# A hybrid decoder layer on one core: small transfers moved to another queue, one product at full width, the last heads laid between the products of the output projection

## The chip, the cores and the metric

One core of a Trainium2 chip runs one launch of the kernel. The metric is the device time of that launch in microseconds (us), the median of several runs. The kernel before takes 2108.51 us (median of 3 runs, 2108.4 to 2108.64).

## The reference, cut to what matters

Everything is fp32. The layer is FFN 1 (SwiGLU), a mixer, FFN 2 (SwiGLU), each behind an RMSNorm that is modulated by a conditioning vector, and a last RMSNorm. The sequence has 256 positions and the model 2048 features. Only the mixer is touched by the change. It has 8 heads of attention with a forget gate (FoX) and 8 heads of a gated delta rule (GDN) in chunks of 64 positions:

```python
def gated_delta_rule(q, k, v, g, beta):      # chunks of 64, n = 4 chunks
    ...
    lower = jnp.where(strict, jnp.einsum("bhnid,bhnjd->bhnij", kb, k) * decay, 0.0)
    t_inv = lax.linalg.triangular_solve(eye + lower, ...)
    u = t_inv @ vb
    w = t_inv @ (kb * jnp.exp(g)[..., None])
    a_intra = jnp.where(incl, jnp.einsum("bhnid,bhnjd->bhnij", q, k) * decay, 0.0)
    def step(state, inp):
        v_new = u_i - w_i @ state
        o = (q_i * jnp.exp(g_i)[..., None]) @ state + a_i @ v_new
        ...
def hybrid_mixer(h, w_in, w_out, ...):
    proj = h @ w_in
    ...
    return jnp.concatenate([o_f, o_g], axis=-1) @ w_out
```

## The kernel before, in words

**Weights.** All weights (674 blocks of 512 KB, eight 128x128 tiles each) come through one class, `Stream` (L68). `next` loads a block on SyncE's queue (L92, SP in the profile), ScalarE (ACT) rounds it to a high part `whi` (L95), and VectorE (DVE) subtracts for the low part `wlo` (L98). Three buffers of each kind go round. `mm` (L351) makes each product of two matmuls: `whi` by both halves of the activation (L352, 512 columns) and `wlo` by the high half (L353, 256 columns); in the mixer's input projection they are L555 to L557 and L568 to L570. Between these blocks the conditioning matrix is read in tiles of 1 MB (L203, `adat`, also on SyncE) and reduced on DVE (L205).

**Order of the work.** The program is written as a sequence of projections (a list of names, `ORDER`, L43: K a key head, G a GDN head, F a FoX head, Z and V row projections). The heads' chains (`solve`, `gdn`, `fox`) are generators: `tick` (L335) goes on with them between products when a planned time has passed, `finish` (L341) runs one to its end. The Tile scheduler then puts every engine's instructions in one fixed list; an engine runs its list in order, so an instruction that waits holds all behind it. That holds for a queue's transfers too.

**The mixer** (L517) first stores the residual stream `x` to DRAM in four transfers of 512 KB (L538, `xd<-x`), uses its space, and reads it back at the end (L542, `x_back`, `x<-xd`). `gates` (L585) stores the decay rows (L642). `row_of` (L650) reads one row broadcast to 128 partitions (L654, `rw<-rowd`, 24 times). `keys` (L689) makes the triangular factor `Ln` of each GDN head (L712). `solve` (L714) inverts the 16x16 diagonal blocks of four heads at once: 8 writes to DRAM (L725, `ld<-Ln`, 8 KB each), 8 broadcast reads (L730, `x<-ld`, 128 KB each), a memset on GpSimd (L734, POOL), 15 pairs of product and sum on DVE (L737, L738). It runs twice.

**`gdn`** (L748): for each of 4 chunks, a product of the packed `wq` with the state (L850), a subtraction (L851, `vz`), a product by `At` (L853), a state update (L857 to L862). `At` holds a_intra transposed, 128x128 for two chunks; L853 multiplies by 64 of its columns, into half of the output's partitions. Then copies of `po` (L866, L867, `orw`), a norm and gate (L875), two transposes (L880, `pot`), and the split to `oh` in high and low (L886, L887).

**The end of the mixer** (L988 to L1007): all chains are finished, `x` is read back, and the output projection runs: 16 output blocks of 128 features, each a sum over 16 heads (`ko`, L994). The first four blocks go together, in four PSUM banks, head by head (64 pairs of matmuls); the others follow one at a time. `residual` (L369, ends at L377) adds each to `x`.

Of the kernel before, what the change touches and what calls it, by code (L numbers as in the profile page):

```python
# [16 lines left out]
P = 128  # L17
D = 2048
T = 256
# [6 lines left out]
NH = 8  # L26
# [13 lines left out]
HIDX = 3  # L40
MORE = True
GAP = {"k": 1.0, "gdn": 1.0, "fox": 1.2}
ORDER = ("K3 K4 K5 K6 K7 Z0 G0 V0 F0 G1 F1 G2 F2 G3 F3 V1 Z1 G4 F4 G5 F5 G6 F6 G7 F7").split()  # L43
N_O = 17
MAGIC = 0x5F3759DF

# [63 lines left out]
def layer_kernel(ctx: ExitStack, tc: tile.TileContext, xt, c, adaw, cols, cst, w, out, order, dbg=None):  # L110
# [76 lines left out]
    def ada_col():  # L187

        i = ada_st["i"]
        if i >= len(ada_seq):  # L190
            return
        ada_st["i"] += 1
        m, j = ada_seq[i]
        q = m * KD + j
        if first_ada:
            t = first_ada.pop(0)
        else:
            t = adap.tile([P, D], F32, name="adat")
            if W.last is None:
                nc.sync.dma_start(t, adaw[i])  # L200
            else:
                with tc.issue_after(W.last):
                    nc.sync.dma_start(t, adaw[i])  # L203
        with W.behind(False):
            V.tensor_tensor_reduce(t, t, cs, 1.0, L("adab", q, 1), ALU.mult, ALU.add, mod[:, q : q + 1])  # L205
        if (m, j) in ada_done:
            ada_done[m, j]()
# [309 lines left out]
    def mixer():  # L517
# [16 lines left out]


        for q in range(4):
            with tc.issue_after(W.last):
                nc.sync.dma_start(xd[:, 4 * q : 4 * q + 4], x[:, 4 * q : 4 * q + 4])  # L538

        def x_back(q):  # L540
            with tc.issue_after(W.last):
                nc.sync.dma_start(x[:, 4 * q : 4 * q + 4], xd[:, 4 * q : 4 * q + 4])  # L542

        def spare(slot, n=2):
            return x[:, slot : slot + n].rearrange("p a t -> p (a t)")
# [39 lines left out]
        def gates(ps):  # L585

            yr = x[:, 8]
            A.copy(yr[R], ps[R])
            y, ny, e, em, t0, q = (x[:, j, : 2 * GR].rearrange("p (t r) -> p t r", t=2) for j in range(10, KD))
            coef = tiny.tile([P, GR], F32, name="coef", bufs=1)  # L590
            tc.keep_in_program_order(A.activation(coef, L("alog"), AF.Exp))
            V.tensor_scalar(coef, coef, -1.0, None, ALU.mult)
            yield 1.0
            pc = psf("pcol")
            pcv = pc[:, : 2 * GR].rearrange("p (t r) -> p t r", t=2)
            for t in range(2):
                PE.transpose(pcv[:, t], yr[R, t * P : (t + 1) * P], ident[R, :GR])
            both = lambda c_: c_.unsqueeze(1).to_broadcast([P, 2, GR])
            V.tensor_tensor(y, pcv, both(L("gbias")), ALU.add)
            V.tensor_tensor(y, y, both(C("sgn")), ALU.mult)  # L600
            V.scalar_tensor_tensor(ny, y, -1.0, y, ALU.mult, ALU.min)
            A.activation(e, ny, AF.Exp)
            V.tensor_scalar(em, y, 0.0, None, ALU.min)
            A.activation(em, em, AF.Exp)

            S = ny
            V.tensor_scalar(t0, e, 2.0, None, ALU.add)
            V.reciprocal(t0, t0)
            V.tensor_tensor(S, e, t0, ALU.mult)
            V.tensor_tensor(t0, S, S, ALU.mult)  # L610
            V.tensor_scalar(q, t0, 1.0 / 17.0, None, ALU.mult)
            for n in (15, 13, 11, 9, 7, 5, 3):
                V.scalar_tensor_tensor(q, q, 1.0 / n, t0, ALU.add, ALU.mult)
            V.scalar_tensor_tensor(q, q, 1.0, S, ALU.add, ALU.mult)
            V.tensor_scalar(y, y, 0.0, None, ALU.max)
            V.scalar_tensor_tensor(y, q, 2.0, y, ALU.mult, ALU.add)
            V.tensor_tensor(y, y, both(coef), ALU.mult)

            V.tensor_scalar(t0, e, 1.0, None, ALU.add)
            V.reciprocal(t0, t0)  # L620
            V.tensor_tensor(colS[:, :, 4], em[:, :, 16:24], t0[:, :, 16:24], ALU.mult)
            yield 6.0

            fox_, gdn_ = slice(0, NH), slice(NH, 2 * NH)
            pr = psf("prow")
            po = psf("pcum")
            pcs = po[:, : 6 * NH].rearrange("p (t q r) -> p t q r", t=2, q=3)
            for t in range(2):
                sl = slice(t * P, (t + 1) * P)
                PE.matmul(pr[:NH, T + t * P : T + (t + 1) * P], y[:, t, gdn_], C("tri64"), start=True, stop=True)  # L630
                PE.matmul(pr[:NH, sl], y[:, t, fox_], C("tri"), start=True, stop=(t == 0))
                if t:
                    PE.matmul(pr[:NH, sl], y[:, 0, fox_], L("ones"), start=False, stop=True)
            for t in range(2):
                PE.matmul(pcs[:, t, 1], C("tri64"), y[:, t, gdn_], start=True, stop=True)
                PE.matmul(pcs[:, t, 2], C("tru64"), y[:, t, gdn_], start=True, stop=True)
                PE.matmul(pcs[:, t, 0], C("tri"), y[:, t, fox_], start=True, stop=(t == 0))
                if t:
                    PE.matmul(pcs[:, t, 0], L("ones"), y[:, 0, fox_], start=False, stop=True)
            rt = x[:, 8:10].rearrange("p a t -> p (a t)")[:NH]  # L640
            A.copy(rt, pr[:NH])
            nc.sync.dma_start(rows, rt)  # L642
            V.tensor_copy(colS[:, :, 0:2], pcs[:, :, 0:2])
            A.activation(colS[:, :, 2:4], pcs[:, :, 1:3], AF.Exp)
            V.tensor_tensor(nbeg, colS[:, :, 4], colS[:, :, 2], ALU.mult)
            V.tensor_scalar(nbt, colS[:, :, 4], -1.0, None, ALU.mult)
            V.tensor_scalar(ng, colS[:, :, 1], -1.0, None, ALU.mult)
            yield 1.0

        def row_of(h, kind, tag):  # L650

            rb = m2p.tile([P, T], F32, name="rw", tag="rw" + tag)
            with tc.issue_after(W.last):
                nc.sync.dma_start(rb, rows[h : h + 1, kind * T : (kind + 1) * T].broadcast_to([P, T]))  # L654
            return rb

        bc = lambda c_: c_.unsqueeze(1).to_broadcast([P, 2, P])
# [56 lines left out]
        def solve(half):  # L714
# [7 lines left out]
            Lh = Ln[:, hs4].rearrange("p h t j -> p (h t) j")  # L722
            for b in range(8):
                r = slice(16 * b, 16 * b + 16)
                nc.sync.dma_start(ld[ht, b].rearrange("n r c -> r n c"), Lh[r, :, r])  # L725
            rows_ = x[:, ht]
            for b in range(8):
                r = slice(16 * b, 16 * b + 16)
                src = ld[ht, b].rearrange("n r c -> n (r c)").unsqueeze(0).to_broadcast([16, n, 256])
                nc.sync.dma_start(rows_[r], src)  # L730
            yield 9.0
            U = tmp.tile([P, n, 16], F32, name="u16", bufs=1)
            pr = tmp.tile([P, n, 16], F32, name="pr16", bufs=1)
# [14 lines left out]
        def gdn(h):  # L748
# [52 lines left out]
            for t in range(2):  # L801
# [3 lines left out]
            U = U2  # L805

            wq = m1p.tile([P, 2, 4, 64], F32, name="wq")
            V.tensor_tensor(wq[:, :, 1:3, :], q_[:, 0].rearrange("p (t c i) -> p t c i", t=2, c=2),
                            egb.rearrange("p (t c i) -> p t c i", t=2, c=2), ALU.mult)
            yield 1.4  # L810
            pu = pss("put")
# [19 lines left out]
                PE.matmul(pu[:, T + t * P : T + (t + 1) * P], kb[:, t], Ub[:, t], start=True, stop=True)  # L831
            u = m1p.tile([P, 2, P], F32, name="u")
            A.copy(uz[:64], pu[:64, :P])
            V.tensor_copy(wq[:, :, 0:4:3, :], pu[:, T:].rearrange("p (t c i) -> p t c i", t=2, c=2))
            A.copy(u.rearrange("p t i -> p (t i)"), pu[:, :T])


# [2 lines left out]
            for c_ in range(4):  # L840
# [5 lines left out]
                if c_ == 0:  # L846
                    new = uz
                else:
                    new = vz[:, c_ - 1]
                    PE.matmul(pc_, wq[:, t, 2 * ev : 2 * ev + 2].rearrange("p a i -> p (a i)"), st, start=True, stop=True)  # L850
                    V.tensor_sub(new[r], u[r, t], pc_[r])  # L851
                    yield 1.2
                PE.matmul(pc_[ro], At[:, t, 64 * ev : 64 * ev + 64], new, start=(c_ == 0), stop=True,  # L853
                          skip_group_check=True)
                if c_ < 3:
                    pst = pss("pst")
                    PE.matmul(pst[:, :P], kd[:, t], new, start=True, stop=True)  # L857
# [5 lines left out]
                    st = s2  # L863
            orw = m1p.tile([P, 2, P], F32, name="orw")
            pov = po.rearrange("p (t c d) -> p t c d", t=2, c=2)
            A.copy(orw[:64], pov[64:, :, 0])  # L866
            A.copy(orw[64:], pov[:64, :, 1])  # L867
            sso = tiny.tile([P, 2], F32, name="sso")
            for t in range(2):
                j1 = tmp.tile([P, P], BF16, name="j1")  # L870
# [114 lines left out]
            have_keys(h, first[1 + h])  # L985
        for name in ORDER:
            step(name[0], int(name[1]))
        for kind in chains:  # L988
            finish(kind, NH)
        for q in range(4):  # L990
            x_back(q)


        ko = [NH + h for h in range(4)] + list(range(NH)) + [NH + h for h in range(4, NH)]  # L994
        for js in [list(range(4))] + [[j] for j in range(4, KD)]:
            pj = [psn(i, "po") for i in range(len(js))]
            for i, k in enumerate(ko):
                for q, j in enumerate(js):
                    mm(pj[q], W.next("o", k, j), oh_[k], i == 0, i == KD - 1)
            for q, j in enumerate(js):  # L1000
                residual(pj[q], j, 5, False)
                sumsq_add(j)
# [139 lines left out]
```

## Time and profile before

| | us |
|---|---|
| median of 3 runs | 2108.51 |
| the profiled execution | 2112.91 |
| its span in the trace | 2111.1 |
| PE busy in the span | 2021.6 (96%) |
| DVE busy | 1564.3 (74%) |
| input projection and heads of the mixer | 806.6 to 1237.87 |
| output projection | 1237.87 to 1345.0 |

PE is TensorE's matmuls and PEld its weight loads, which overlap them; ACT is ScalarE, DVE VectorE, POOL GpSimd, SP SyncE. A row of the groups has line, engine, operation, output and inputs, shapes and count, then busy time and mean ns of one, then the idle time of the engine ahead of it and who ended it. A row of the timeline has the start, the length (both us), engine, line, operation, names, count, and in brackets the idle time before it and who ended that. The mean granted TensorE clock was 0.983 over the span. A row of the windows gives, for a stretch of the span in us, each engine's busy time with its instructions in brackets, the granted clock, and the load of the DMA engines.

### The profile page before, as it was taken

To read this page: it belongs to the slowest core of one execution; us is meant where nothing else is said; L and a number is where in the kernel's file an instruction comes from. 1 tells how busy PE (TensorE), PEld (TensorE's weight loads), DVE (VectorE), ACT (ScalarE), POOL (GpSimd) and SP (SyncE) were. 2 spreads that over 40 slices of the span, in tenths; PEclk is the share of its full clock that TensorE was granted. 3 is DMA by queue.
4 is the path that set the end of the run, shared out by engine and by line. 5 is a ranking of instruction groups with operands and counts; after the bars stand their busy time and mean duration, and the time that the engine had idled before them with its cause. 6 is when DMAs were issued, how large, how long until landed. Compare 5 with 4: busy or idle time off the path is not lost.

```text
span 2111.1 us, 33297 instructions
## 1 busy us (share of the span) xinstructions
PE 2021.6 (96%) x12914; PEld 1822.2 (86%) x12914; DVE 1564.3 (74%) x2387; ACT 1021.2 (48%) x1583; POOL 59.3 (3%) x62
## 2 busy tenths in 40 slices
PE   4999999999999998879999999899999999999997
PEld 4998999888888888769989988788888888888886
DVE  6899877888888887877877878776665555555554
ACT  4544444333444446646656654454444334444442
POOL 0000000000000020000000002000000000000011
PEclk9999999999999999999999999999999999999998
DMA  8989777999998984676566657576766555555553
GB/s 309 333 338 354 261 258 242 333 343 337 327 336 328 335 305 154 194 241 236 191 230 229 226 184 283 186 258 232 237 229 200 189 190 190 190 190 189 190 190 110
DMA packets 129344, 521.26 MB, mean 247 GB/s; under 512 B 16409, under 2 KB 21529, under 8 KB 110753
## 3 DMA queue, kind: packets, MB, share of 16 engines
q1 hardware_dynamic: 129186, 519.13, 70.1%
q8 instruction: 101, 1.65, 0.3%
q14 instruction: 57, 0.47, 0.1%
HBM read 514.74 MB, written 4.34 MB: 246 GB/s over the span
## 4 chain that ended last, share of the span: by engine, by line
PE 85%; DVE 6%; DMA 4%; issue 2%; ACT 1%; SPq 1%; POOL 0%; DVEq 0%; ACTq 0%; POOLq 0%
PE pd L352 14%; PE pg L352 11%; PE pu L352 11%; PE pd L353 7%; PE pg L353 5%; PE pu L353 5%; PE pgu L424 4%; PE pgu L422 4%; PE pgu L423 4%; PE pp L555 3%; PE pp L557 3%; PE pp L556 3%; DMA adat<-in_ada_dram 3%; PE po L352 2%; DVE wlo L98 2%
## 5 line engine op out<-in xcount | busy, mean ns | idle before, releaser
L98 DVE TENSOR_TENSOR wlo<-wraw,whi 128x1024 fp32r<-128x1024 f32 x674 | 821.6, 1224 | 343.5 <-ACT whi L95 342.1
L95 ACT CAST whi<-wraw 128x1024 fp32r<-128x1024 f32 x674 | 705.5, 1049 | 761.6 <-PE pd L352 218.0
L352 PE MATMUL pd<-hid,whi 128*128 128x512 f32 x1408 | 492.3, 393 | 0.0
L353 PE MATMUL pd<-hid,wlo 128*128 128x256 f32 x1408 | 393.4, 280 | 1.3 <-DVE wlo L98 1.2
L205 DVE CUSTOM_DVE_ANT_0 adat<-adat,cs,colt 128x2048 f32<-128x2048 f32 x140 | 332.5, 2375 | 64.5 <-DMA adat<-in_ada_dram 63.9
L352 PE MATMUL pg<-hs,whi 128*128 128x512 f32 x960 | 339.6, 394 | 2.1 <-DVE hs L295 1.8
L352 PE MATMUL pu<-hs,whi 128*128 128x512 f32 x960 | 340.0, 395 | 0.0
L352 PEld LDWEIGHTS pd<-hid,whi 128*128 128x128 f32 x1408 | 263.7, 187 | 61.9 <-DVE hid L367 0.3
L353 PE MATMUL pu<-hs,wlo 128*128 128x256 f32 x960 | 269.4, 281 | 0.0
L353 PE MATMUL pg<-hs,wlo 128*128 128x256 f32 x960 | 269.2, 281 | 0.0
L353 PEld LDWEIGHTS pd<-hid,wlo 128*128 128x128 f32 x1408 | 264.4, 188 | 2.3 <-DVE wlo L98 2.3
L422 PE MATMUL pgu<-hs,whi 128*128 128x256 f32 x896 | 255.9, 287 | 7.4 <-ACT whi L95 6.3
L424 PE MATMUL pgu<-hs,wlo 128*128 128x256 f32 x896 | 252.3, 287 | 7.6 <-DVE wlo L98 7.4
L423 PE MATMUL pgu<-hs,whi 128*128 128x256 f32 x896 | 255.0, 286 | 0.0
L352 PEld LDWEIGHTS pg<-hs,whi 128*128 128x128 f32 x960 | 180.5, 188 | 43.5 <-issue 2.1
L352 PEld LDWEIGHTS pu<-hs,whi 128*128 128x128 f32 x960 | 180.4, 188 | 41.5
L555 PE MATMUL pp<-hs,whi 128*128 128x256 f32 x656 | 193.9, 296 | 9.5 <-ACT whi L95 8.3
L557 PE MATMUL pp<-hs,wlo 128*128 128x256 f32 x656 | 188.6, 287 | 2.4 <-DVE wlo L98 2.2
L556 PE MATMUL pp<-hs,whi 128*128 128x256 f32 x656 | 188.2, 287 | 0.0
L353 PEld LDWEIGHTS pg<-hs,wlo 128*128 128x128 f32 x960 | 181.8, 189 | 0.5 <-DVE wlo L98 0.4
L353 PEld LDWEIGHTS pu<-hs,wlo 128*128 128x128 f32 x960 | 181.8, 189 | 0.1
L422 PEld LDWEIGHTS pgu<-hs,whi 128*128 128x128 f32 x896 | 174.2, 195 | 8.7 <-ACT whi L95 7.0
(284 smaller groups left out, 2407.4 us busy)
## 6 DMA issues: line engine op xcount, KB each, us to landing
wraw<-in_w_dram SPq DMA_DIRECT2D x674, 512.0 KB, 4.4
adat<-in_ada_dram SPq DMA_DIRECT2D x140, 1024.0 KB, 7.3
adaf<-in_ada_dram SPq DMA_DIRECT2D x4, 1024.0 KB, 12.6
rw<-rowd SPq DMA_DIRECT2D x24, 128.0 KB, 4.1
xd<-x SPq DMA_DIRECT2D x4, 512.0 KB, 6.4
x<-ld SPq DMA_DIRECT2D x16, 128.0 KB, 5.2
x<-xd SPq DMA_DIRECT2D x4, 512.0 KB, 5.1
out_dram<-o SPq DMA_DIRECT2D x8, 256.0 KB, 2.2
```

The lines of the kernel that those rows point to most:

```text
L95: nc.scalar.copy(self.h, r)
L98: nc.vector.tensor_tensor(self.l, r, self.h.bitcast(F32), ALU.subtract)
L205: V.tensor_tensor_reduce(t, t, cs, 1.0, L("adab", q, 1), ALU.mult, ALU.add, mod[:, q : q + 1])
L352: PE.matmul(ps, wt[0], act.rearrange("p a t -> p (a t)"), start=first, stop=False)
L353: PE.matmul(ps[:, :T], wt[1], act[:, 0], start=False, stop=last)
L422: PE.matmul(o, wh, hs[:, k, 0], start=first and s == 0, stop=False, skip_group_check=skip)
L423: PE.matmul(o, wh, hs[:, k, 1], start=False, stop=False, skip_group_check=skip)
L424: PE.matmul(o, wl, hs[:, k, 0], start=False, stop=last, skip_group_check=skip)
L555: PE.matmul(pp[i][:, :T], wh, hs[:, k, 0], start=(k == 0), stop=False)
L556: PE.matmul(pp[i][:, :T], wh, hs[:, k, 1], start=False, stop=False)
L557: PE.matmul(pp[i][:, :T], wl, hs[:, k, 0], start=False, stop=(k == KD - 1))
```

## The change

Three edits, all in the mixer.

1. **Small transfers.** The four `xd<-x`, the four `x<-xd`, the decay rows' store, the 24 `rw<-rowd`, the 16 `ld<-Ln` and the 16 `x<-ld` are issued by GpSimd (`nc.gpsimd.dma_start`) and no longer by SyncE. The wait behind the last weight load (`issue_after(W.last)`) goes with them. SyncE issues weights and `adat` alone.
2. **At.** L853 multiplies by all 128 columns of `At` into all 128 output partitions. The order of the four parts of `wq` is changed for it (q outside, w inside), and the halves that L851 and the copies L866 and L867 read.
3. **The end.** The chains are no longer finished ahead of the output projection: in front of each head's products only that head's own chain is finished, and `tick` goes on with the others between products. `ko` ends with FoX 6, FoX 7 and GDN 7. G7 stands before F6 in `ORDER`. `x_back` is called after the products of the first four blocks.

```diff
-ORDER = ("... G5 F5 G6 F6 G7 F7").split()
+ORDER = ("... G5 F5 G6 G7 F6 F7").split()
...
-            with tc.issue_after(W.last):
-                nc.sync.dma_start(xd[:, 4 * q : 4 * q + 4], x[:, 4 * q : 4 * q + 4])
+            nc.gpsimd.dma_start(xd[:, 4 * q : 4 * q + 4], x[:, 4 * q : 4 * q + 4])
         def x_back(q):
-            with tc.issue_after(W.last):
-                nc.sync.dma_start(x[:, 4 * q : 4 * q + 4], xd[:, 4 * q : 4 * q + 4])
+            nc.gpsimd.dma_start(x[:, 4 * q : 4 * q + 4], xd[:, 4 * q : 4 * q + 4])
...
-            with tc.issue_after(W.last):
-                nc.sync.dma_start(rb, rows[h : h + 1, ...].broadcast_to([P, T]))
+            nc.gpsimd.dma_start(rb, rows[h : h + 1, ...].broadcast_to([P, T]))
...
-                nc.sync.dma_start(ld[ht, b].rearrange("n r c -> r n c"), Lh[r, :, r])
+                nc.gpsimd.dma_start(ld[ht, b].rearrange("n r c -> r n c"), Lh[r, :, r])
...
-                nc.sync.dma_start(rows_[r], src)
+                nc.gpsimd.dma_start(rows_[r], src)
...
-            V.tensor_tensor(wq[:, :, 1:3, :], q_[:, 0]...
+            V.tensor_tensor(wq[:, :, 0:4:3, :], q_[:, 0]...
...
-            V.tensor_copy(wq[:, :, 0:4:3, :], pu[:, T:]...
+            V.tensor_copy(wq[:, :, 1:3, :], pu[:, T:]...
...
-                    V.tensor_sub(new[r], u[r, t], pc_[r])
+                    V.tensor_sub(new[r], u[r, t], pc_[ro])
                     yield 1.2
-                PE.matmul(pc_[ro], At[:, t, 64 * ev : 64 * ev + 64], new, start=(c_ == 0), stop=True,
-                          skip_group_check=True)
+                PE.matmul(pc_, At[:, t], new, start=(c_ == 0), stop=True, skip_group_check=True)
...
-        for kind in chains:
-            finish(kind, NH)
-        for q in range(4):
-            x_back(q)
-        ko = [NH + h for h in range(4)] + list(range(NH)) + [NH + h for h in range(4, NH)]
+        ko = [NH + h for h in range(4)] + list(range(6)) + [NH + h for h in range(4, 7)] + [6, 7, NH + 7]
         for js in [list(range(4))] + [[j] for j in range(4, KD)]:
             pj = [psn(i, "po") for i in range(len(js))]
             for i, k in enumerate(ko):
+                finish("gdn" if k >= NH else "fox", k % NH)
                 for q, j in enumerate(js):
                     mm(pj[q], W.next("o", k, j), oh_[k], i == 0, i == KD - 1)
+                    tick(TILE_US)
+            if js[0] == 0:
+                for q in range(4):
+                    x_back(q)
```

More of the change, by code (lines that the diff above doesn't have):

```diff
@@ L42 @@
 GAP = {"k": 1.0, "gdn": 1.0, "fox": 1.2}
-ORDER = ("K3 K4 K5 K6 K7 Z0 G0 V0 F0 G1 F1 G2 F2 G3 F3 V1 Z1 G4 F4 G5 F5 G6 F6 G7 F7").split()
+ORDER = ("K3 K4 K5 K6 K7 Z0 G0 V0 F0 G1 F1 G2 F2 G3 F3 V1 Z1 G4 F4 G5 F5 G6 G7 F6 F7").split()
 N_O = 17
@@ L198, in ada_col @@
             t = adap.tile([P, D], F32, name="adat")
-            if W.last is None:
+            with tc.issue_after(W.last):
                 nc.sync.dma_start(t, adaw[i])
-            else:
-                with tc.issue_after(W.last):
-                    nc.sync.dma_start(t, adaw[i])
         with W.behind(False):
@@ L641, in gates @@
             A.copy(rt, pr[:NH])
-            nc.sync.dma_start(rows, rt)
+            nc.gpsimd.dma_start(rows, rt)
             V.tensor_copy(colS[:, :, 0:2], pcs[:, :, 0:2])
@@ L652, in row_of @@
             rb = m2p.tile([P, T], F32, name="rw", tag="rw" + tag)
-            with tc.issue_after(W.last):
-                nc.sync.dma_start(rb, rows[h : h + 1, kind * T : (kind + 1) * T].broadcast_to([P, T]))
+            nc.gpsimd.dma_start(rb, rows[h : h + 1, kind * T : (kind + 1) * T].broadcast_to([P, T]))
             return rb
@@ L807, in gdn @@
             wq = m1p.tile([P, 2, 4, 64], F32, name="wq")
-            V.tensor_tensor(wq[:, :, 1:3, :], q_[:, 0].rearrange("p (t c i) -> p t c i", t=2, c=2),
+            V.tensor_tensor(wq[:, :, 0:4:3, :], q_[:, 0].rearrange("p (t c i) -> p t c i", t=2, c=2),
                             egb.rearrange("p (t c i) -> p t c i", t=2, c=2), ALU.mult)
@@ L833, in gdn @@
             A.copy(uz[:64], pu[:64, :P])
-            V.tensor_copy(wq[:, :, 0:4:3, :], pu[:, T:].rearrange("p (t c i) -> p t c i", t=2, c=2))
+            V.tensor_copy(wq[:, :, 1:3, :], pu[:, T:].rearrange("p (t c i) -> p t c i", t=2, c=2))
             A.copy(u.rearrange("p t i -> p (t i)"), pu[:, :T])
@@ L865, in gdn @@
             pov = po.rearrange("p (t c d) -> p t c d", t=2, c=2)
-            A.copy(orw[:64], pov[64:, :, 0])
-            A.copy(orw[64:], pov[:64, :, 1])
+            A.copy(orw[:64], pov[:64, :, 0])
+            A.copy(orw[64:], pov[64:, :, 1])
             sso = tiny.tile([P, 2], F32, name="sso")
```

## The prediction

> **What bounds the kernel now.** I read the engine totals first, then the windows of the mixer, then PE's waits and, at those waits, the timeline of SyncE's queue.
>
> ```profile
> PE 2021.6 (96%) x12914; PEld 1822.2 (86%) x12914; DVE 1564.3 (74%) x2387; ACT 1021.2 (48%) x1583; POOL 59.3 (3%) x62
> ```
> ```profile
> 862.20:981.30 119.10, 100.93 (x609) 87.12 (x608) 92.12 (x231) 64.28 (x131) 0.63 (x2) 0.93 0.69 219
> 883.30:931.00 47.70, 31.03 (x165) 26.58 (x165) 37.67 (x110) 20.44 (x30) 0.63 (x2) 0.82 0.77 233
> 931.00:981.30 50.30, 50.22 (x330) 43.98 (x330) 38.88 (x70) 27.32 (x54) 0.00 (x0) 1.00 0.66 246
> 981.00:1238.00 257.00, 255.50 (x1896) 236.97 (x1896) 208.39 (x470) 158.49 (x335) 0.00 (x0) 1.00 0.62 218
> 1238.00:1278.00 40.00, 35.62 (x205) 29.27 (x204) 26.80 (x70) 18.04 (x38) 0.00 (x0) 0.91 0.65 224
> ```
>
> PE is busy for 96% of the span: time can be won only where PE has gaps, runs at a low clock, or has matmuls that take longer than they must. The windows show two places. In 862.2:981.3 PE is busy 100.93 of 119.10 us, so 18.2 us are gaps, nearly all in 883.3:931. From 981 to 1238 it is full (255.50 of 257.00). In 1238:1278, the first four blocks of the output projection, 4.4 us are gaps. PE's waits in 862:931 name who ended the gaps:
>
> ```profile
> PE pp L555 <- ACT whi L95: 8.3, 1, 8.3
> PE pv L568 <- ACT whi L95: 5.2, 1, 5.2
> PE pp L557 <- DVE wlo L98: 2.2, 1, 2.2
> PE pv L569 <- DVE wlo L98: 1.8, 3, 0.8
> ```
>
> All four are weight blocks that came late. SyncE's queue shows why:
>
> ```profile
> 865.64 0.33 SPq L92 DMA_DIRECT2D wraw<-in_w_dram  x1
> 868.91 1.04 SPq L654 DMA_DIRECT2D rw<-rowd  x2
> 872.06 3.65 SPq L725 DMA_DIRECT2D ld<-Ln  x8
> 875.75 4.67 SPq L730 DMA_DIRECT2D x<-ld  x8
> 880.53 0.37 SPq L654 DMA_DIRECT2D rw<-rowd  x1
> 881.00 0.37 SPq L92 DMA_DIRECT2D wraw<-in_w_dram  x1
> ...
> 896.65 3.64 SPq L725 DMA_DIRECT2D ld<-Ln  x8
> 900.38 3.70 SPq L730 DMA_DIRECT2D x<-ld  x8
> ...
> 904.99 0.35 SPq L92 DMA_DIRECT2D wraw<-in_w_dram  x1
> ```
>
> The queue is in order. Between 865.64 and 881.00 it issues no weight block: it waits for the factor `Ln`, then issues the solve's 16 transfers at about half a microsecond each. The second solve does the same from 896.65 to 904.99. A gap costs once more, in the clock: 0.82 in 883.3:931. There a matmul takes 31.03/165 = 0.188 us against 50.22/330 = 0.152 us in the next stretch; 165 x 0.036 = 5.9 us, with a mix of shapes that isn't the same, so I take 4 us. The two solves cost 18 + 4 = **22 us**.
>
> **Part 1, small transfers on GpSimd.** It takes 22 us of loss away if weights are all that SyncE waits for. But the blocks must still pass ACT and DVE, and the solve still needs its transfers. DVE has 92.12 us of work in the stretch, PE 119.1 - 22 = 97. With so little between them, a few late instructions on DVE or ACT reach PE, and not all 22 come back.
>
> The instruction lists of the two programs as built tell what stands where. In the changed one the first solve's steps move on DVE from behind block 286 to behind block 295; the last `Ln` it needs is at block 284, so its transfers have 11 blocks of cover (3 before). The second goes from block 291 to 304 with `Ln` at 296: 8 blocks. What a block takes on PE comes from the plain output projection, where the matmuls of L352 are one per product:
>
> ```profile
> 1278.00:1340.00 62.00, 61.92 (x178) 33.11 (x178) 1.00 0.73 275
> ```
>
> 62.0/178 = 0.348 us for a product, 2.8 us for a block of eight. The cover is 30 us and 22 us. What must fit into it:
>
> ```profile
> x<-ld SPq DMA_DIRECT2D x16, 128.0 KB, 5.2
> ld<-Ln SPq DMA_DIRECT2D x16, 8.0 KB, 1.5
> L252 POOL TENSOR_TENSOR sqacc<-sqacc,sq x42: 732/1167/1603, 722.0 to 2089.2; 128x256 f32<-128x256 f32 x42
> 886.15 0.31 POOL L734 MEMSET x<- 128x128 f32 x1 [86.37 <-DMA rw<-rowd]
> ```
>
> No transfer is issued by POOL in the trace, so its price p is unknown. SyncE's 3.65/8 = 0.46 us is the lower end; POOL's own instructions take 0.31 (memset) to 1.60 us (sums), and I take 1.2 us, the median of its sums: that is the instruction of which its row shows most (42 of 62), and it lies well inside the two ends. A solve then takes 16 x 1.2 + landings of 1.5 + 5.2 = 26 us: inside the first cover, 4 us beyond the second, where DVE would wait. The weight buffers (three) hold two blocks, 5.6 us, ahead of PE, so I charge 2 us. That POOL holds its queue in order too matters little: behind the solve's transfers stand only broadcasts `rw`, the memset and the other solve. Three of the four stores of `x` stand between POOL's sums in FFN 1, the fourth behind the last; POOL is busy for 3% of the span and one sum comes with each output block, so a store of p finds room. I cost them at nothing; if one stood in the way of the last sum it would cost p, 1.2 us.
>
> The new order has a price on ACT. Between the casts of blocks 296 and 297 five activation-table loads stand in a row with the `silu` and `exp` work that the old stalls spread out:
>
> ```profile
> L667 ACT ACT_TABLE_LOAD x3 | 3.8, 1283 | 0.1
> L705 ACT ACTIVATE j<-pk 128x128 bf16<-128x128 f32 x10 | 2.6, 271 | 3.5 <-PE pk L699 3.5
> L95 ACT CAST whi<-wraw 128x1024 fp32r<-128x1024 f32 x15 | 15.6, 1045 | 12.9 <-DVE u L738 6.9 <-DMA wraw<-in_w_dram 4.8 <-PE pp L556 1.0
> ```
>
> Five loads are 6.4 us and a dozen activations at 0.3 about 4 us: some 10 us, and the next cast 1.05. Two blocks in hand cover 5.6, which leaves 6 us of wait for PE and, by the proportion above (4 us of clock for 18 of gaps), 1.5 to 2 us of clock. Part 1 is -22 + 2 + 6 + 2 = **-12 us**; ends -20 (ACT fits) and +2 (DVE as late as now).
>
> **Part 2, At at full width.**
>
> ```profile
> 1250.30 0.43 PE L853 MATMUL po<-vz,At 128*64 128x128 f32 x2
> 1250.66 0.49 PE L857 MATMUL pst<-vz,kbd 128*128 128x128 f32 x2
> 1250.90 0.48 PE L352 MATMUL po<-oh,whi 128*128 128x512 f32 x1
> ```
> ```profile
> 1250.66 0.30 PEld L857 LDWEIGHTS pst<-vz,kbd 128*128 128x128 f32 x2 [0.17 <-issue]
> ```
> ```profile
> L853 PEld LDWEIGHTS po<-vz,At x48: 132/134/137, 947.2 to 1254.7; 128*64 128x64 f32 x48
> L850 PEld LDWEIGHTS po<-st,wq x48: 186/191/192, 946.0 to 1253.9; 128*128 128x128 f32 x48
> ```
>
> One L853 product is two passes. From its start to the next product's is 1250.66 - 1250.30 = 0.36 us, while L857, two passes at full width, takes 0.24; the weight load behind L853 starts 0.17 us late and waits for nothing that the profile shows. There are 64/2 = 32 such products: 32 x 0.12 = **-4 us** if the lateness belongs to the change of width. The other end: wider loads, (0.191 - 0.134) x 64 = +3.6 us where nothing hides them. I take -4, since L850 and L857 already have the wide load and no lateness. The row's 0.134 and 0.191 us bear out in direction a rule that speaks against this edit: the Trainium skill (TensorE: Matmul & The Clock Gate, § LDWEIGHTS) has a load's time grow with the columns loaded; by the rule alone this part would be a loss of 3.6 us. Subtractions and copies keep their number and size: nothing.
>
> **Part 3, the end.**
>
> ```profile
> PE pot L880 <- DVE orw L875: 3.3, 1, 3.3
> ```
> ```profile
> 1258.58 0.61 DVE L875 SCALAR_TENSOR_TENSOR orw<-orw,rsy_o,x 128x128 f32<-128x128 f32 x2
> 1260.71 0.48 DVE L887 SCALAR_TENSOR_TENSOR oh<-pot,colt,oh 128x256 fp32r<-128x256 f32 x1 [1.51 <-ACT oh L886]
> ```
> ```profile
> x<-xd SPq DMA_DIRECT2D x4, 512.0 KB, 5.1
> ```
>
> In the old list `pot` stands behind 37 of the first 128 output matmuls, and PE stops 3.3 us there for `orw`. In the new one it stands behind 120, so that gap goes, with the others of this window (4.4 us) and some 1.7 us of its clock (0.91): -6 us. What is late next: only the four products of GDN 7 stand behind `pot`, and they need its `oh`; from the end of L875 to the end of L887 DVE shows 2.0 us, in part `pot` itself, so +1.5. Then `x_back`: the residuals wait for the read of part 0, which can leave only when `orw` is done (GDN 4 to 7 read their gate from that space). Issue 1.2 + landing 5.1 after `orw`, against about 2 us for `pot` and the last products: the residual starts 4 us late, and the fifth block needs a PSUM bank that this residual frees: +4 us (ends +2 and +8). Part 3 is -6 + 1.5 + 4 = **-0.5 us**; ends -6 and +4.
>
> **The sum.** -12 - 4 - 0.5 = -16.5 us: 2112.91 (the span of 2111.1 and 1.8 around it) becomes 2096.4 in a profiled execution. The profiled one stands 4.4 us above the median of the runs, so I carry the difference over: 2108.51 - 16.5 = **2092.0 us**.
>
> **The rivals.**
>
> *Slower: GpSimd issues too slowly.* Mechanism: both solves' transfers run past their cover and the DVE steps behind them hold all `wlo`. Lost on PE: (16p + 6.7 - 30 - 5.6) + (16p + 6.7 - 22.4 - 5.6) = 32p - 50.6 us, where each bracket counts if positive. It eats the 18.5 us that the sum has without its 2 us of DVE wait from p = 69.1/32 = 2.2 us on; at p = 2.5 the time is 18.5 - 29.4, that is 11 us slower, 2119. For it: no row of POOL shows a transfer. Against it: no sum of POOL takes over 1.6 us. The Trainium skill (SBUF — State Buffer, § SBUF: two separate sides) has a rule for it: DVE instructions that hold both ports keep GpSimd from writing descriptors, 3.1 us instead of 0.62 in its measurement; no run so far shows it, and with 3.1 in place of p the formula gives +30 us.
>
> *The stall only moves.* DVE and ACT bound the stretch: at 92.12 us of work plus the new waits, 862:981 keeps 15 or more of its 22 us. Part 1 is then -4, the sum -8.5, 2100; if nothing is left of part 1, -4.5 us, 2104.
>
> *At gains nothing.* The late load may come from the order of the partitions, or the wide load may be exposed: part 2 is +3.6, the sum -9, 2099.5. With the rival above, the two together give about -1 us, no change.
>
> *It doesn't do what it says.* The lists exclude that for the queue and for the end; for the width too.
>
> **How the numbers follow.** A difference below 0.2%, 4.2 us, can't be told from no change. My forecast, a gain of 11 to 24 us, has a chance of 0.45; a moved stall or an At without gain, leaving 4.3 to 11 us, 0.20; the two together or a cheap form of the slow issue, within 4.2 us either way, 0.13; slow issue at 2.3 us or more, or a longer wait for `x` at the end beside a moved stall, 0.22. So faster 0.65, same 0.13, slower 0.22. The range goes from 2083 (-25.5: part 1 at -20, the others at -5 together) to 2114 (+5.5: p near 2.3), and leaves out some 0.05 below and 0.15 above.
>
> **What would show it.** Right: no gap on SyncE's queue of weight loads; POOL transfers 1.2 us apart; PE full in 866:931 but for one wait of about 6 us on `whi` of block 297; L853 with no late load behind it, 0.24 us each; no wait of `pot`; a wait of PE or DVE for `x<-xd` of some 4 us near 1260. Wrong: a wait of DVE's L737 on POOL or on `x<-ld` of 10 us or more at a solve; PE gaps of 15 us or more in the old places with ACT or DVE named.

## The result, and the profile after

The changed kernel takes 2123.26 us (median of 4 runs, 2120.67 to 2126.49) beside 2108.57 for the kernel before: a ratio of 1.0066, 95% interval 1.0048 to 1.0084. Timed a second time it was 1.0051 (1.0036 to 1.0066). It is 11 to 14 us **slower**; the forecast was 16.5 us faster, and the time lies above the range. Below, "us slower" for an experiment is its ratio to the runs of the kernel before that were made beside it, times 2110 us.

First, where the time goes. The input projection has 784 products that read a `wlo` tile, in both kernels in one order; I compared when the same product starts, from the first one on (differences of starts in the two traces). In the kernel before, the stalls of the two solves stand at products 160 and 184.

| product | before, us | after, us | after is |
|---|---|---|---|
| 0 | 807.8 | 805.6 | |
| 176 | 904.0 | 898.9 | 2.8 ahead |
| 192 | 923.0 | 905.4 | 15.4 ahead |
| 272 | 970.0 | 970.2 | 2.4 behind |
| 384 | 1023.0 | 1029.6 | 8.8 behind |
| output projection starts | 1237.9 | 1245.1 | 9.4 behind |
| its first four blocks done | 1278.2 | 1284.1 | 8.1 behind |
| its last product done | 1345.3 | 1353.4 | 10.3 behind |

So both stalls went from their old places and 15 us were won, nearly all of it at the second one: behind the first, at product 176, the changed kernel is only 2.8 us ahead. By product 272 the 15 us were lost again, with 6 more by product 384; the end, where 6 us were to be gained and 5.5 given back, stayed about as it was. The page and the windows of the changed kernel (columns as before), cut at product 192, past 272 and at the output projection:

```profile
PE 2022.5 (95%) x12914; PEld 1828.6 (86%) x12914; DVE 1558.3 (73%) x2387; ACT 1020.2 (48%) x1583; POOL 92.8 (4%) x127
...
rw<-rowd POOLq DMA_DIRECT2D x24, 128.0 KB, 3.7
xd<-x POOLq DMA_DIRECT2D x4, 512.0 KB, 7.3
x<-ld POOLq DMA_DIRECT2D x16, 128.0 KB, 5.5
x<-xd POOLq DMA_DIRECT2D x4, 512.0 KB, 6.1
```
```profile
804.30:906.00 101.70, 94.87 (x657) 86.93 (x658) 77.02 (x185) 72.99 (x148) 15.91 (x30) 0.97 0.68 207
906.00:970.00 64.00, 51.61 (x293) 43.22 (x292) 46.56 (x119) 32.00 (x55) 9.84 (x19) 0.89 0.65 204
970.00:1245.10 275.10, 266.76 (x2009) 253.82 (x2008) 219.33 (x507) 161.26 (x349) 5.48 (x10) 0.99 0.61 214
1245.10:1284.10 39.00, 31.75 (x186) 27.39 (x185) 25.70 (x64) 16.41 (x34) 2.15 (x4) 0.88 0.71 246
```

PE is missing 12.4 us in 906:970 (and the clock falls to 0.89), 8.3 in 970:1245, where the kernel before was full but for 1.5 us, and 7.3 in the first output blocks. From 981 on, where the kernel before waits 1.0 us in all, PE's waits name chains of heads (a line has the us in all, the times and the longest):

```profile
PE pft L929 <- DVE on L925: 5.7, 4, 2.5
PE pot L873 <- DVE orw L868: 1.2, 1, 1.2
```

These are transposes that stand in PE's list and wait for a norm on VectorE. VectorE's own waits in 850:1240, first of the kernel before, then of the changed one, have one large new entry:

```profile
DVE dec L665 <- DMA rw<-rowd: 2.3, 3, 1.3
```
```profile
DVE dec L659 <- DMA rw<-rowd: 15.4, 9, 3.0
```

The decay mask `dec` waits for its row 9 times, 15.4 us in all. One of these waits, in the timelines of VectorE and of GpSimd:

```profile
1010.93 0.35 DVE L855 SCALAR_TENSOR_TENSOR st<-st,rw,pst 128x128 f32<-128x128 f32 x1
1016.36 0.43 DVE L659 TENSOR_TENSOR dec<-cstt,rw 128x256 f32<-128x256 f32 x1 [3.05 <-DMA rw<-rowd]
```
```profile
1011.57 0.55 POOL L648 DMA_DIRECT2D rw<-rowd  x1 [30.54 <-DVE st L855]
```

The rows of the GDN heads have two buffers, and a head holds its row until its last state update (`st`, L855). The next row but one can be read only then: GpSimd issues it 0.3 us behind `st`, it has landed by 1016.4, and VectorE was at the mask by 1013.3. In the lists the mask of G2 to G7 stands at most one weight block behind the `st` that frees its buffer (304 and 304, 318 and 319, 327 and 328, 337 and 338, 358 and 359, 366 and 367); in the kernel before, where the row is issued on SyncE behind a weight load, it is 5 to 21 blocks behind (302 and 316, 318 and 325, 327 and 348, 336 and 356, 358 and 365, 367 and 372). With the rows on the free queue the scheduler put the mask, with its wait, where nothing covers the transfer; the run with only the rows moved, below, has the masks within two blocks of it too.

### The profile page after: what moved, and what is told of

Read it like the earlier page. It is cut to its first block, busy times and chain, and to the rows that moved or that the text cites. A ratio compares the mean times of both kernels' runs of the same rounds, so it can differ in the third digit from the quotient of the medians.

```text
span 2120.6 us, 33322 instructions
## 1 busy us (share of the span) xinstructions
PE 2022.5 (95%) x12914; PEld 1828.6 (86%) x12914; DVE 1558.3 (73%) x2387; ACT 1020.2 (48%) x1583; POOL 92.8 (4%) x127
## 4 chain that ended last, share of the span: by engine, by line
PE 74%; DVE 9%; DMA 9%; issue 5%; ACT 2%; POOL 0%; DVEq 0%; SPq 0%; ACTq 0%; POOLq 0%
PE pd L349 15%; PE pg L349 10%; PE pu L349 10%; PE pd L350 8%; PE pg L350 5%; PE pu L350 5%; DMA adat<-in_ada_dram 5%; DVE wlo L98 3%; PE pgu L421 2%; PE pgu L419 2%; PE po L349 2%; PE pgu L420 2%; PE pp L550 2%; DMA wraw<-in_w_dram 2%; PE pp L551 2%
```

## The experiments

The theory, **R**: the rows' masks, moved up behind the updates, make VectorE wait, and it passes the wait on to the heads' chains and to `wlo`. The rival, **S**: the solves, whose steps now stand 9 to 13 blocks later, push all chains back. A third, **E**, came up for the end. The 12 runs follow; each part alone first.

**Part 1 alone.**

> Part 1 alone (all small transfers on GpSimd; At at 64 columns and the end as before). Theory R (the read of the decay row): the list of the changed kernel puts each head's decay mask right behind the last state update of the head before, whose buffer it needs, so VectorE waits some 3 us for each row's landing; with At's gain of 4.5 us missing and the end's loss of about 4 missing too, this run is like the changed kernel, 2123 us, plus or minus 3. Theory S (the solves): the loss comes only from the solves' steps placed 9 to 13 weight blocks later: the same 2123 here; the runs with one of the two alone tell these apart. If part 1 were not the place of the loss: 2100 or less.

2117.8 us, 1.0034 (1.0022 to 1.0046): 7 us slower, less than expected. VectorE waited 13.6 us for rows. Part 1 loses, but it isn't all: with the two other parts, each run alone below, the sum is under 1 us slower (7.2 - 2.5 - 4.2), against 11 to 14 together. The rest comes only from the parts in one program. (The buffer that is needed is that of the head two before, not of the head before.)

**Part 3 alone**, transfers on SyncE.

> Part 3 alone (the last heads between the output products, GDN 7 ahead of FoX 6, the read of x behind the first four blocks; transfers on SyncE, At at 64 columns). From the changed kernel's profile, where the first four blocks and the step to the fifth take about 4 us more than before: 2112, plus or minus 2. If the end gains as its removed wait says and only GpSimd's queue made it late: 2105.

2109.54 us, 0.9988 (0.9973 to 1.0002): no loss, and no clear gain; the time lies between the two that were expected. In its trace the first four blocks took 33.4 instead of 40.3 us. The loss at the end is not part 3's own.

**Only the rows on GpSimd.**

```diff
-            with tc.issue_after(W.last):
-                nc.sync.dma_start(rb, rows[...])
+            nc.gpsimd.dma_start(rb, rows[...])
```

> Only the 24 reads of decay rows go to GpSimd, all else as before; the solves keep their places in VectorE's list (behind blocks 286 and 291). Theory R: the masks stand right behind the state updates here too, VectorE waits 10 to 15 us in all for these rows, and the time is 2114 to 2122. Theory S: the solves have not moved, SyncE's queue is a little shorter, 2106 to 2109.

2114.99 us, 1.0016 (1.0007 to 1.0026): 3.4 us slower, with the solves within a few blocks of their old places (behind blocks 287 and 288). VectorE waited 12.5 us for rows. R's direction, at the low end of what it expected; S alone is contradicted, since it gave no loss here. Whether it was the queue or the dropped wait behind the last weight load that had kept the masks back, no run separates.

**The changed kernel with a third buffer for these rows.**

```diff
-            rb = m2p.tile([P, T], F32, name="rw", tag="rw" + tag)
+            rb = m2p.tile([P, T], F32, name="rw", tag="rw" + tag, bufs=3 if tag == "g" else 2)
```

> The changed kernel with a third buffer for the decay rows of the GDN heads (one number), so that a row can be read one head earlier and need not wait for the last state update; the solves stay at blocks 295 and 304. Theory R: VectorE's waits for rows fall from 15 us to below 5, and the time to 2112 to 2116. Theory S: unchanged, 2121 to 2125.

2112.52 us, 1.0008 (0.9997 to 1.0018) where the changed kernel has 1.0066 and 1.0051: 9 to 12 us of the loss is gone with 1 KB of each partition, the queues unchanged. VectorE's waits in 850:1240:

```profile
DVE dec L659 <- DMA rw<-rowd: 2.9, 2, 2.5
```

The solves were not moved back, so it is the rows' two buffers that cost these 9 to 12 us. But it is not shown that the time went the way R says, through waits on VectorE: the waits past 970, 6.8 us of the 15.4, are gone, and the stretch past product 272 is no shorter (278.8 us, 275.1 in the changed kernel). What is shorter is the stretch from product 192 to 272, by 8 us, where ScalarE's table loads stand (see the jam below). With the third buffer its list has a cast between them, at 917.84, where the changed kernel has none from 910.80 to 920.73:

```profile
917.53 0.40 ACT L663 ACTIVATE rw<-rw 128x256 f32<-128x256 f32 x1
917.84 1.03 ACT L95 CAST whi<-wraw 128x1024 fp32r<-128x1024 f32 x1
918.89 1.28 ACT L679 ACT_TABLE_LOAD   x1
```

**The changed kernel again, beside the next three.**

> The changed kernel once more, unaltered, so that it is timed on the same chip as the three runs beside it and against the same runs of the kernel before: 10 to 16 us slower than before by all theories.

2121.73 us, 1.0051 (1.0036 to 1.0066).

**Part 2 alone.**

> Part 2 alone (At at full width, all else as before). By the changed kernel's trace a pair of L853 matmuls now takes 0.22 us instead of 0.36: 32 x 0.14 = 4.5 us less than before. If part of it is hidden or given back: 0 to 2 less.

2106.02 us, 0.998 (0.9971 to 0.999): 4.2 us faster.

**Parts 2 and 3.**

> Parts 2 and 3 without part 1. If the parts add up: the 4.5 us of At and the 2.5 us that part 3 alone gained (its trace says 4.5 in the first four blocks), together 7 to 9 us less than before. If part 3 itself carries the late end of the changed kernel: 0 to 3 less.

2102.54 us, 0.9966 (0.9955 to 0.9977): 7.2 us faster. Without part 1 the change gains.

**The changed kernel with the read of `x` back on SyncE.** In its trace the last head's norm on VectorE is cut in two:

```profile
1268.36 0.15 DVE L225 TENSOR_TENSOR rsa_o<-rsy_o 128x2 f32<-128x2 f32 x1
1271.04 2.35 DVE L202 CUSTOM_DVE_ANT_0 adat<-adat,cs,colt 128x2048 f32<-128x2048 f32 x1 [2.53 <-DMA adat<-in_ada_dram]
1273.31 0.08 DVE L202 DVE_READ_ACCUMULATOR2_ANT mod<- 128x1 f32 x1
1273.31 0.15 DVE L226 SCALAR_TENSOR_TENSOR rsa_o<-rsa_o,sso 128x2 f32<-128x2 f32 x1
...
1274.91 0.62 DVE L868 SCALAR_TENSOR_TENSOR orw<-orw,rsy_o,x 128x128 f32<-128x128 f32 x2
```

These rows are of the changed kernel: between two steps of one reciprocal root, the list has a reduction of the conditioning matrix, which first waits 2.53 us for its tile.

> The changed kernel with only the four reads of x at the end of the mixer back on SyncE's queue, behind the last weight load. Theory E (order of the end): with these reads gone from SyncE, a tile of the conditioning matrix is loaded earlier, and its reduction stands on VectorE inside the last head's norm, where it waits 2.5 us for its transfer and takes 2.4 more; put back, the reduction stands behind that norm as in part 3 alone, the first four blocks take some 34 instead of 39 us, and the time is 5 us below the changed kernel beside it. Rival: GpSimd's read of x is itself late (its landing is 6.1 us against 5.1): then 1 us at most.

2114.56 us, 1.0016 (1.0005 to 1.0027), 7 us below the changed kernel beside it. Its timeline has the reduction behind `orw`, and the window of its first four blocks is 32.2 instead of 39.0 us:

```profile
1271.70 0.61 DVE L869 SCALAR_TENSOR_TENSOR orw<-orw,rsy_o,x 128x128 f32<-128x128 f32 x2
1273.36 2.35 DVE L202 CUSTOM_DVE_ANT_0 adat<-adat,cs,colt 128x2048 f32<-128x2048 f32 x1
```
```profile
1247.70:1279.90 32.20, 30.32 (x186) 26.44 (x185) 25.64 (x64) 14.40 (x31) 0.00 (x0) 0.98 0.73 257
```

E holds: the loss at the end comes from what the emptied SyncE queue let the scheduler put earlier on VectorE. PE's wait for `x` (3.3 us in the changed kernel) goes with it, since that read can leave only behind `orw`; GpSimd's later landing (6.1 against 5.1 us) is about 1 us of this at most.

**Parts 2 and 3 with the solves' transfers on GpSimd.**

> Parts 2 and 3, and of part 1 only the solves' transfers (16 writes and 16 reads) on GpSimd; rows and x on SyncE. VectorE's list has the solves behind blocks 295 to 302 and 305 to 310, with no mask among them that waits for a late row. Theory R (rows): freed from the 18 us of gaps at the two solves, this run is 3 to 8 us faster than parts 2 and 3 alone, 0.993 to 0.995 of before. Theory S (the solves' later place gives all back): no faster than parts 2 and 3 alone (0.9966), or slower.

2100.09 us, 0.9947 (0.9932 to 0.9962): 11 us faster than before, the fastest of all runs, 4 us below parts 2 and 3 (the two intervals overlap slightly, and each has its own runs of before). Of part 1 the piece that takes the transfers out of the weights' way gains, where S expected no gain. But S's cost is in it too: beside parts 2 and 3 it is 17 us faster up to product 192 and loses 11 of them by product 272. PE still waits for late weight blocks, in 850:1240:

```profile
PE pv L568 <- ACT whi L95: 8.0, 3, 6.3
PE pv L569 <- DVE wlo L98: 4.8, 5, 2.0
```

**The changed kernel with the solves' transfers back on SyncE.**

> The changed kernel with only the solves' transfers back on SyncE (rows, the stores and the reads of x stay on GpSimd). Theory R: VectorE's waits for rows stay above 10 us and the time within 4 us of the changed kernel, 2118 to 2124. Theory S: 8 us or more below it, 2113 or less.

2121.92 us, 1.0053 (1.0037 to 1.007): the loss stays, against what S expected. VectorE's wait for rows is 19.9 us. This doesn't clear the solves of their cost: in the traces (the table at the end of this section) the run is 20.7 us slower than the changed kernel up to product 192, where the old stalls are back, and 19.1 us faster from there to product 272. In the changed kernel, moving the solves cost as much as it gained.

**Both mends together**, third buffer and read on SyncE.

> The changed kernel with both mends, the third row buffer and the read of x on SyncE. If these two are what the change lost, and they are independent: the change's 1.006 less some 0.005 for the rows and 0.0035 for the end, 0.996 to 0.998 of before, near parts 2 and 3 without part 1 (0.9966). If a third loss remains: 1.000 or above.

2103.33 us, 0.9965 (0.9952 to 0.9978). The two losses make up what separates the changed kernel from a gain: 1.0066 or 1.0051 becomes 0.9965, 18 to 21 us. That is no more than parts 2 and 3 give (0.9966): even mended, part 1 as a whole is worth nothing.

**Parts 2 and 3 with the solves' transfers on ScalarE's queue.**

> Parts 2 and 3, and the solves' transfers on ScalarE's queue, which holds neither the weights nor a mask. The steps stay behind blocks 285 to 296. If only the place of the transfers on SyncE made the 18 us of gaps: 5 to 15 us faster than parts 2 and 3 alone. If ScalarE's queue then holds the casts while it waits for the factors: as parts 2 and 3 alone or slower, the waits on weight blocks staying at 10 us or more.

2111.95 us, 1.0004 (0.9992 to 1.0016): the 7 us of parts 2 and 3 are lost. ScalarE's list has the transfers in one piece; the first solve's reads, which need the writes to have landed, go out from 876.86 to 887.31, and the copies stand behind them. PE's longest wait in 840:1240 is for one of those copies:

```profile
872.60 3.49 ACTq L725 DMA_DIRECT2D ld<-Ln  x7
876.86 10.45 ACTq L730 DMA_DIRECT2D x<-ld  x8
```
```profile
PE pkk L702 <- ACT kk L706: 11.9, 1, 11.9
```

A queue with the casts and copies in order behind it was no place for transfers that wait.

**Where the time stands, run by run.** The same stretches in the traces, in us; the repeat of the changed kernel differs from it by 2.1 us at most in any of them.

| run | product 0 to 192 | 192 to 272 | 272 to the output projection | its first to last product |
|---|---|---|---|---|
| before | 115.2 | 47.0 | 268.1 | 106.9 |
| only the rows on GpSimd | 116.2 | 46.6 | 271.6 | 107.1 |
| parts 2 and 3 | 115.6 | 45.9 | 267.3 | 99.8 |
| parts 2 and 3, solves on GpSimd | 98.7 | 56.9 | 269.0 | 100.4 |
| changed | 99.8 | 64.8 | 275.1 | 107.8 |
| changed, third buffer | 99.1 | 56.8 | 278.8 | 107.4 |
| changed, read on SyncE | 100.3 | 64.2 | 274.3 | 99.7 |
| changed, solves on SyncE | 120.5 | 45.7 | 273.6 | 108.1 |

The rows alone cost 3.5 us past product 272 and little elsewhere: that is R as it was told. The moved solves gain 16 to 17 us up to product 192 and cost 10 to 11 by product 272 even with the rows left on SyncE: S was right about that cost. With both moved the stretch from 192 to 272 loses 18, and a third buffer takes 8 of these back. Why the stretch past product 272 stays 7 to 12 us longer than with parts 2 and 3 in the kernels with both moved is open; with the third buffer, PE waits 4.5 us at 970 for a `cv` whose steps stand on VectorE among the second solve's.

## Why the prediction was wrong

**The bound: right. The two stalls, -22: -15.4.** Both are gone from their old places, and product 192, behind both, starts 15.4 us earlier. In the kernel before PE lacks 18.2 us up to it, in the changed one still 6.8, in shorter waits for late blocks near the first solve. The rival "the stall only moves" was nearer to what came than the sum: of these 15.4 us none was left by product 272.

**The price of a transfer on GpSimd: too high, and harmless.** Taken as 1.2 us, it is less than half of that, next to SyncE's 0.46:

```profile
870.85 3.70 POOL L719 DMA_DIRECT2D ld<-Ln  x7 [0.24 <-DVE rsa_k L222]
877.68 0.53 POOL L719 DMA_DIRECT2D ld<-Ln  x1 [3.13 <-DMA rw<-rowd]
878.38 4.27 POOL L724 DMA_DIRECT2D x<-ld  x8 [0.17 <-issue]
...
914.99 4.20 POOL L719 DMA_DIRECT2D ld<-Ln  x8 [2.78 <-DVE u L732]
920.83 4.18 POOL L724 DMA_DIRECT2D x<-ld  x8 [1.64 <-DMA ld<-Ln]
```

4.27/8 = 0.53 us. So the slower case that the prediction priced, a slow issue from 2.2 us on, did not happen; the sign came from another cause. (The two brackets of that case add up to 32p - 50.2, not 50.6; the bound of 2.2 us stays.) The Trainium skill (SBUF — State Buffer, § SBUF: two separate sides) has a transfer from GpSimd take 0.62 us alone and 3.1 us beside a VectorE copy that holds the shared ports. VectorE ran no copy beside the second solve's transfers (914.99 to 925.01), so this trace doesn't show that case; the issues there took 0.53 us, with VectorE busy for 46.56 of 64 us in 906:970.

**The step that failed first: "That POOL holds its queue in order too matters little: behind the solve's transfers stand only broadcasts `rw`".** The rows were priced at nothing, as transfers. What was held in GpSimd's queue itself did matter little: the second solve's memset stood behind a row's read that waited 28.78 us for `st`, but VectorE waited only 0.6 us for that memset.

```profile
953.79 0.58 POOL L648 DMA_DIRECT2D rw<-rowd  x1 [28.78 <-DVE st L855]
954.36 0.34 POOL L728 MEMSET x<- 128x128 f32 x1
```

What counts is the rows' consumer. The prediction followed the solves and the end through the lists, not the masks, which move up to within a block of the `st` that frees their row. Measured: 15.4 us of waits on VectorE, and 9 to 12 us of the time come back with a third buffer. By the traces the rows cost 3.5 us alone, and 8 us are what the third buffer takes back at the jam that follows.

**The jam on ScalarE: right in place, 10 us forecast, 17.8 lost.** Forecast 6 us of wait, 2 for the second solve and 2 of clock. The five table loads stand where they should, from 910.80 to 920.41, and PE's gaps at 921.82 and 925.32 are 4.59 and 2.28 us. But the jam reaches back to SyncE. Its queue, and then ScalarE:

```profile
914.38 0.42 SPq L200 DMA_DIRECT2D adat<-in_ada_dram  x1
925.29 10.12 SPq L92 DMA_DIRECT2D wraw<-in_w_dram  x4
```
```profile
910.80 1.28 ACT L661 ACT_TABLE_LOAD   x1
912.81 1.28 ACT L679 ACT_TABLE_LOAD   x1
914.90 1.28 ACT L661 ACT_TABLE_LOAD   x1
917.39 1.28 ACT L679 ACT_TABLE_LOAD   x1 [0.49 <-DVE cv L678]
919.12 1.28 ACT L663 ACT_TABLE_LOAD   x1
...
932.75 1.05 ACT L95 CAST whi<-wraw 128x1024 fp32r<-128x1024 f32 x1 [8.19 <-DMA wraw<-in_w_dram]
```

While ScalarE is held, no weight buffer comes free, so no weight block is issued from 914.38 to 925.29, and the cast after the jam waits 8.19 us for one. (The last 2 us of this are VectorE's: a buffer is free when VectorE has subtracted, and its list has a reduction of the conditioning matrix, 921.06 to 923.40, ahead.) From product 192 to 272, 17.8 us are lost (15.4 ahead, then 2.4 behind). Before and after, between these two products:

```profile
923.00:970.00 47.00, 46.92 (x295) 40.31 (x294) 37.72 (x67) 24.55 (x45) 0.00 (x0) 1.00 0.66 244
```
```profile
905.40:970.20 64.80, 52.41 (x300) 43.95 (x299) 46.76 (x120) 32.02 (x55) 9.84 (x19) 0.89 0.65 206
```

Some 12 us are gaps and 5.5 are PE's time for nearly the same matmuls at a granted clock of 0.89. With a third row buffer, or with the rows on SyncE, the same stretch loses 9.8 or 9.9 us, what the forecast had: the term was about right for the solves, and lacked what the rows do to it.

**At: right.** -4 forecast, -4.2 measured alone. The row of its weight loads now reads (48 of them; 16 more, of `uz`, have a row of their own)

```profile
L847 PEld LDWEIGHTS po<-vz,At x48: 186/189/192, 949.5 to 1264.2; 128*128 128x128 f32 x48
```

and the next product starts, in the median of the 32, 0.22 us after its own (0.14 to 0.33; 0.36 before in 31 of 32), as here, 1257.23 - 1257.01:

```profile
1257.01 0.38 PE L847 MATMUL po<-vz,At 128*128 128x128 f32 x2
1257.23 0.39 PE L850 MATMUL pst<-vz,kbd 128*128 128x128 f32 x2
```

The load itself did grow (0.134 to 0.189 us), as the Trainium skill's rule on columns has it (TensorE: Matmul & The Clock Gate, § LDWEIGHTS); the lateness behind the narrow load was worth more.

**The end: the sum came out by accident.** The forecast was -6 (the gap of `pot` and others goes), +1.5 (`oh`) and +4 (wait for `x`). The waits of the changed kernel in 1245:1360:

```profile
PE po L349 <- DVE x L374: 3.3, 1, 3.3
PE pot L873 <- DVE orw L868: 2.8, 1, 2.8
...
PE po L349 <- DVE oh L880: 1.1, 1, 1.1
```

The waits for `x` (3.3) and `oh` (1.1) are near what was priced, but `pot` still waits 2.8 us. The failed term is the -6: `pot` stands as far back as the list said, but `orw` itself is late by the reduction in its norm. With that put right by the read on SyncE, the first four blocks take 32 us, 8 less than before, with 1.9 us of gaps.

The chance of 0.22 for slower was given to one mechanism, a price, and to a longer wait at the end. Neither made it slower: changed lists did, at the rows' masks with ScalarE's jam behind them, and at the reduction in the last norm. With both mended the kernel is 7 us faster, still 9 short of the 16.5: part 1, -12 in the sum, then gives nothing.

## What to carry to other kernels

Where a scheduler fixes the lists, moving a transfer to an idle queue moves its consumers as well: look up where the consumer's instruction now stands against the one that frees the transfer's buffer, on every engine, and count the transfer's landing as a wait if less work than that lies between. A busy queue can be what keeps a consumer at a safe distance; here, when it was emptied, a further buffer gave the distance back. A stall that has gone from its place may stand further on: compare when the same product starts in both traces, behind the old place and behind the new one. Take a change apart and keep the parts that gain: here parts 2 and 3 with the solves' transfers alone were 11 us faster, while the whole was 11 to 14 slower.

## What the runs showed of the hardware

A transfer issued by GpSimd took its queue 0.53 to 0.57 us in the median of each kind (changed kernel), against 0.30 to 0.43 on SyncE (kernel before), for a write of 8 KB as for a broadcast of 128 KB. Landings were alike for small ones, 3.7 against 4.1 us for the rows, 5.5 against 5.2 for `x<-ld`, and about 1 us longer for the copies of 512 KB (7.3 against 6.4, 6.1 against 5.1). I had reckoned with more than twice that issue time. In the kernel before, the two-pass fp32 matmul of L853, which loads 64 columns of its stationary operand, held the next weight load up by 0.17 us in 31 of 32 cases, 0.36 us a pair; at 128 columns with a longer load the pair took 0.22 in the median. The count of columns alone isn't the reason: behind the transposes of L760, which load 64 columns too, the next load comes at once (0.09 us late at most). What is, no run here separates.
